# A three-branch decoder trunk: a scan that starts later, values that meet other scores, and four transposes in one bank

## The chip, the cores and the metric

The kernel runs on one core of a Trainium2 chip. The metric is device time in microseconds (us) of one execution. The core has TensorE (PE, matmuls, with PEld for its weight loads), VectorE (DVE), ScalarE (ACT), GpSimd (POOL) and SyncE (SP), and DMA queues that SP, ACT and POOL issue to. Each engine works through its own list of instructions in order and waits where a tile isn't ready.

## What is computed

Two layers, each on a stream x of 256 tokens by 1024 channels. One combined projection of the normalised stream feeds three causal mixers; each has its own SiLU gate path, is projected back, and the three are merged by sigmoid gates, projected and added to x. Cut to what matters:

```python
for layer in range(2):
    h = rms_norm(x, norm_w[layer])
    proj = einsum('bsd,de->bse', h, w_in[layer])             # 1024 -> 12832
    (a_xbc, a_z, a_dt, b_q, b_k, b_v, b_z, c_q, c_k, c_v, c_f, c_z, gates) = split(proj)
    y_a = mamba2_branch(a_xbc, a_z, a_dt, ...)               # conv, scan in chunks of 128, 16 heads of 64 in 4 groups
    y_b = sliding_window_branch(b_q, b_k, b_v, b_z, ...)     # window 128, 16 heads, 4 kv heads, sinks
    y_c = forgetting_attention_branch(c_q, c_k, c_v, c_f, c_z, ...)   # 16 heads, decaying scores
    branch = einsum('bsiw,iwd->bsid', stack(y_a, y_b, y_c), w_proj[layer])
    g = sigmoid(gates + gate_bias[layer])
    x = x + einsum('bsd,de->bse', sum(g * branch), w_out[layer])
return rms_norm(x, final_norm_w)

def scan_of_a_group(x, dt, a, B, C):                         # two chunks
    x_dt = x * dt
    decay = exp(a_cum[l] - a_cum[s]) where l >= s
    y_diag = (C B^T * decay) x_dt                            # inside a chunk
    y_off  = C * state of the chunk before * exp(a_cum)      # across the chunks
    return y_diag + y_off
```

All is float32. The kernel's names: branch 0 is the scan (mamba2), branch 1 the sliding-window attention (swa), branch 2 the forgetting attention (fox). z is a branch's gate path.

## The kernel before, in words

**Matmuls.** Every projection is computed in a split of float32 into a high and a low part: three products (hi·hi, lo·hi, hi·lo) per 128 rows of the contraction. Weights stream from memory in pieces of 512 KB on SP's queue into tiles `raw`; ACT makes `hi` (L291) and DVE makes `lo` (L292), a few pieces ahead of PE (AHEAD 4). The smaller products (scores, values, transposes, the scan) are plain float32.

**The order of PE** is written by a planner that runs while the program is built. A list `ops` holds the projections of a layer in a fixed order: the sequence in the main loop from L1255 on, with `heavy` (eight convolution pieces of the scan's inputs), `lights` (one lighter piece behind each), `z1` (gate paths), and `gates_proj(br)` (two merge gates `g` and two output projections `p` of a branch). Between projections, and in the middle of wide ones, `pump` (L149) takes steps of generators from the list `waiting`: one generator for each quad of attention heads (`swa_quad`, `fox_quad`, both through `attn_quad`), and one `ssd_group` (L853) for each of the scan's four groups. A generator yields a number (planner microseconds until its next step), a condition, a token's name, or `Half(...)`. The planner's clock advances by an estimate for each matmul; `pump` takes at most 1.35 us of steps at a time. `Half` marks a step whose matmuls use only half of PE's array (64 columns or 64 rows). Such steps are held until another one is near (`early`, within MEET 5 us), and if one is taken the others that are ready follow without regard to the budget. `drain(br)` runs a branch's generators to their end.

**Other engines** aren't ordered by the planner but by a scheduler that lets whatever is ready go first. Tiles of one tag share a few buffers; a tile gets its buffer in the order of the program's first writers. The tags that matter: `L4` has two buffers (the scan's broadcasts, the fox attention's turned probabilities `two`, the swa's `first`), `L2` eight (gates, `xdt`, the decays and others), `mx` five PSUM banks. Tokens: one for prepared probabilities (`pp`), one for a group between its preparation and the end of its values (`ssd`), two for broadcasts (`bcg`).

**A group of the scan** (`ssd_group`). It waits until all swa generators are gone, takes a `bcg` token, and issues on ACT's queue a broadcast of its four rows of cumulated decay rates to all partitions (L857, 512 KB). After D_BC and with the `ssd` token it transposes its x into `mx` banks, two transposes to a bank, and DVE multiplies each bank by dt into `xdt` (L866). Then DVE and ACT make `ds` (L869, L870), and the decays `dec` (L879, L881) and `cross` (L885, the last reader of the broadcast). D_SSD later PE makes the products of C and B, DVE multiplies the decays by them (L894). The next yield is `Half(D_SSD2)`, and then come 24 matmuls of 64 columns, the group's values (`py`, L906).

**Fox attention** (`attn_quad`). A quad's scores go to four `mx` banks, DVE and ACT make probabilities, six transposes, a pause, six transposes; ACT copies each bank of four (L696) to `two` and one more tile; then value products (L712), which two quads do together, beside the next quad's scores.

**Constants of a layer** (`layer_consts`, `layer_vec`). Layer 1 loads them on POOL's queue at its start, layer 2 on ACT's at the end of layer 1. The rows dt_bias, f_bias, sinks, a_log and d_skip (16 values each) go to one partition (`y.hr`); a matmul with ones spreads them to 128 partitions, ACT copies them to `y.hb`.

**Order of the gates of branch 1.** In layer 1 the gate piece (1,0) is projected early in the layer, (1,1) behind the fifth heavy piece, and the projection (p,0) behind the eighth. In layer 2 gate 0 comes behind the fifth, projection 0 behind the eighth, then gate 1 and projection 1.

Of the kernel before, what the change touches and what calls it, by code (L numbers as in the profile page):

```python
# [13 lines left out]
AF = mybir.ActivationFunctionType  # L14
ALU = mybir.AluOpType

P = 128
# [9 lines left out]
D_GN1, D_GN2, D_CUM, D_H, D_M = 8.0, 13.5, 17.0, (4.8, 6.4), 5.0  # L27
BUDGET = 1.35
T_PP, T_SSD, T_BIAS = 1, 1, 1
D_FOLD = 8.0  # L30
N_RAW, N_SPLIT = 6, 6
AHEAD = 4
# [16 lines left out]
def hybrid_trunk(  # L49
# [17 lines left out]
    def T(tag, shape, dtype=F32, bufs=None):  # L67
        count[0] += 1
        return sb.tile(shape, dtype, tag=tag, name=f"{tag}_{count[0]}",
                       bufs=bufs if bufs is not None else BUFS.get(tag, 1))  # L70
# [8 lines left out]
    def pmx():  # L79
        return PS("mx", 5)  # L80
# [28 lines left out]
    def transpose(o, a, i):  # L109
        clock["t"] += 0.109  # L110
        nc.tensor.transpose(o, a, i)  # L111
# [36 lines left out]
    def pump(budget=BUDGET):  # L148
        t0 = clock["t"]  # L149
        half = False  # L150
        while True:
            over = clock["t"] - t0 >= budget
            if over and not half:
                return
            for m in sorted(waiting, key=lambda m: (m[0], m[1])):
                if ready(m) and (m[5] if over else not early(m)):
                    half = m[5]
                    enter(m)
                    break
            else:  # L160
                return
# [123 lines left out]
    def pin(f):  # L285
        return lambda *a, **k: tc.keep_in_program_order(f(*a, **k))
# [145 lines left out]
    def layer_consts(y, queue):  # L432
        l = y.l
        pdma = pin(queue.dma_start)
        both = T("L1", [88, 2 * P])
        vr, y.hr = both[:, 0:P], both[0:1, P:P + 80]
        pdma(vr[0:64, :], conv_w[l].rearrange("j (u p) -> (j u) p", p=P))
        pdma(vr[64:80, :], conv_b[l:l + 1, :].rearrange("o (u p) -> (o u) p", p=P))
        pdma(vr[80:88, :], ssm_norm_w[l:l + 1, :].rearrange("o (u p) -> (o u) p", p=P))
        if l:  # L440
            y.nwb = T("nwb", [P, D])
            pdma(y.nwb, norm_w[l:l + 1, :].to_broadcast([P, D]))
            pin(nc.gpsimd.tensor_scalar)(y.nwb, y.nwb, -0.5, None, op0=ALU.mult)

        for i, v in enumerate((dt_bias, f_bias, sinks, a_log, d_skip)):
            pdma(y.hr[:, 16 * i:16 * i + 16], v[l:l + 1, :])
        y.vr = vr

    def layer_vec(y):
        p = pmx()  # L450
        transpose(p[:, 0:88], y.vr, ident[:88, :88])
        y.vec = T("vec", [P, 88], bufs=2)
        mm(p[:, 96:176], ones[0:1, :], y.hr, start=True, stop=True)
        y.hb = T("hb", [P, 80], bufs=2)
        pin(act)(y.hb, p[:, 96:176], AF.Copy)
        pin(act)(y.vec[:, 0:80], p[:, 0:80], AF.Copy, scale=0.5)
        pin(act)(y.vec[:, 80:88], p[:, 80:88], AF.Copy, scale=-0.5)
        y.nega = T("nega", [P, 16], bufs=2)
        pin(act)(y.nega, y.hb[:, 48:64], AF.Exp)
        gts = nc.gpsimd.tensor_scalar  # L460
        y.nsink = T("nsink", [P, 16], bufs=2)
        gts(y.nsink, y.hb[:, 32:48], -1.0, None, op0=ALU.mult)
        gts(y.nega, y.nega, -1.0, None, op0=ALU.mult)
        y.dsk = T("dsk", [P, NK], bufs=2)
        for i in range(2):
            r = slice(64 * i, 64 * i + 64)
            nc.gpsimd.tensor_copy(y.dsk[r, :], y.hb[r, 64:80].rearrange("p (j i) -> p i j", i=2)[:, i, :])
# [384 lines left out]

    def ssd_group(y, g):  # L853
        yield lambda: not any(m[2] == 1 for m in waiting)
        yield "bcg"
        bcg = T("L4", [P, 4, S])
        nc.scalar.dma_start(bcg, y.cumd[1, 4 * g:4 * g + 4, :].partition_broadcast(P))  # L857
        yield D_BC
        yield "ssd"
        xdt = T("L2", [P, 2, 256])  # L860
        hs = slice(4 * g, 4 * g + 4)
        for t in range(2):
            p = pmx()
            for j in range(2):
                transpose(p[:, j * P:(j + 1) * P], y.xs[:, 2 * g + j, t * P:(t + 1) * P], ident)
            tt(xdt[:, t, :].rearrange("p (h d) -> p h d", h=4),  # L866
               p[:, 0:256].rearrange("p (h d) -> p h d", h=4), bc(y.dt[:, t, hs], 2, 64), op=ALU.mult)
        ds = T("ds", [P, 4], bufs=2)
        tt(ds, bcg[:, :, P - 1], y.acum[:, 0, hs], op=ALU.subtract)  # L869
        act(ds, ds, AF.Exp)  # L870
        xds = T("L1", [P, 256])
        tt(xds.rearrange("p (h d) -> p h d", h=4), xdt[:, 0, :].rearrange("p (h d) -> p h d", h=4),
           bc(ds, 2, 64), op=ALU.mult)
        decs = []
        for c in range(2):
            tk = slice(c * P, (c + 1) * P)
            dec = T("L2", [P, 4, P])
            for h in range(4):
                stt(dec[:, h, :], bcg[:, h, tk], y.acum[:, c, 4 * g + h:4 * g + h + 1], negtri,  # L879
                    op0=ALU.subtract, op1=ALU.add)  # L880
            act(dec, dec, AF.Exp)  # L881
            decs.append(dec)

        cross = T("L2", [P, 4, P])
        act(cross, bcg[:, :, P:S], AF.Exp)  # L885
        decs.append(cross)
        yield D_SSD
        tokens["bcg"] += 1

        p = pmx()  # L890
        mm(p[:, 0:S], y.bcT[:, g, 0:P], y.bcT[:, 4 + g, :], start=True, stop=True)
        mm(p[:, S:3 * P], y.bcT[:, g, P:S], y.bcT[:, 4 + g, P:S], start=True, stop=True)
        for dec, c in zip(decs, (0, 2, 1)):
            tt(dec, dec, bc(p[:, c * P:(c + 1) * P], 1, 4), op=ALU.mult)  # L894
        yield Half(D_SSD2)

        py = pmx()
        for c in range(2):
            for j in range(2):
                o = py[:, S * j + P * c:S * j + P * c + P]  # L900
                for s in range(c + 1):
                    for i in range(2):
                        h = 2 * j + i
                        hc = slice(64 * h, 64 * h + 64)
                        a, b = (xdt[:, c, hc], decs[c][:, h, :]) if s == 0 else (xds[:, hc], cross[:, h, :])
                        mm(o[64 * i:64 * i + 64, :], a, b, start=(s == 0), stop=(s == c))  # L906
        for j in range(2):
            u = 2 * g + j
            stt(y.xs[:, u, :], y.xs[:, u, :], y.dsk[:, u:u + 1], py[:, S * j:S * j + S], op0=ALU.mult, op1=ALU.add)
        yield D_SSD3  # L910
        tokens["ssd"] += 1
# [337 lines left out]
    for y in layers:  # L1249
# [27 lines left out]
        def gates_proj(br):  # L1277
            def g(b):
                c = 512 * b
                op(cols(C_G + D * br + c, 512), u_gate(y, br, c, 0), u_gate(y, br, c, 1))  # L1280

            def p(b):
                c = 512 * b
                if b == 0 and br != 0:
                    op(None, lambda y=y: split_late(y, br))
                i = sub([(0, w_proj[l, br, :, c:c + 512])], 512)
                if br == 0:
                    op(i, u_proj_normed(y, c, 0), u_proj_normed(y, c, 1))
                else:
                    op(i, u_proj(y, br, c, 0), u_proj(y, br, c, 1))  # L1290
            seq = [(g, 0), (p, 0), (g, 1), (p, 1)]
            if br == 1 and l == 0:

                seq = [(g, 0), (g, 1), (p, 0), (p, 1)]
            if br == 0:

                seq = [(lambda b: z1(C_ZA, 0, b), b) for b in range(4)] + [(g, 0), (g, 1), (p, 0), (p, 1)]
            return [lambda f=f, b=b: f(b) for f, b in seq]

        gp = gates_proj(1)  # L1300
        if l == 0:
            v, cv0, cv1 = cols(C_BV), cols(C_CV), cols(C_CV + 256)
            op(v, *(u_bv(y, t, first) for t in range(2)))
            op(None, lambda: layer_consts(y0, nc.gpsimd))
            op(None, lambda: launch(9, normalize(y0), 0.0))
            op(cv0, u_cv(y, 0, 0), u_cv(y, 0, 1))
            op(cv1, u_cv(y, 256, 0), u_cv(y, 256, 1))
            gp.pop(0)()
            op(None, lambda: tables(fin["rope"]))
            op(None, lambda: normalized(y0))  # L1310
        else:
            cv0, v = cols(C_CV, 512), cols(C_BV)
            op(None, lambda: drain(5))
            op(cv0, u_cv(y, 0, 0))
            op(v, u_bv(y, 0))
            op(None, lambda: drain(6))
            op(cv0, u_cv(y, 0, 1))
            op(v, u_bv(y, 1))
        op(rcols(C_BK), *u_bk(y))
        for g in range(4):  # L1320
            op(rcols(C_BQ + 256 * g), *u_bq(y, g))
# [242 lines left out]
```

## Time and profile before

| | |
|---|---|
| three runs | 1197.9, 816.55, 814.36 us; median 816.55 |
| the profiled execution | 815.95 us, span 814.2 us, granted PE clock 0.998 |
| PE busy | 803.2 us, 99% |
| DVE, ACT, POOL busy | 684.4, 534.4, 157.4 us |
| DMA | 170.35 MB, mean 209 GB/s |
| scan broadcasts | 8 of 512 KB, issued at 165.51, 165.89, 185.41, 202.14 in layer 1 and 554.28, 554.65, 574.77, 593.05 in layer 2 |

A profile page gives busy times for each engine, and then the span in 40 slices, one digit each, in tenths of busy time. The waits view lists what an engine waited for: total us, times, longest. Timelines list instructions: start, duration, engine, line, operation, output from inputs, array tile, shape; a bracket at the end is the idle time before and what ended it. Matmul durations overlap, so on PE the distance from one start to the next counts. L107 and L111 are the helpers through which all matmuls and all transposes go; a row's names and shapes tell which step it is.

### The profile page before, as it was taken

What the parts mean: (1) busy time and instruction counts of PE and PEld (TensorE: products, weight loads), DVE (VectorE), ACT (ScalarE), POOL (GpSimd) and SP (SyncE); (2) the same over time, 40 slices, a digit from 0 to 9 for tenths busy, and PEclk for the clock granted to TensorE, in tenths of its full rate; (3) what the DMA queues carried; (4) which work ended last, traced back from release to release, by engine and by line L of the source; (5) the groups of instructions that cost most, each with busy time, mean ns of one, the idle gap of its engine ahead of it and who ended that gap; (6) DMA issues with size and microseconds to landing.
All of it is one profiled execution on the core that took longest, in us unless ns stands there. A gap on an engine that the chain in (4) does not pass through costs nothing.

```text
span 814.2 us, 14891 instructions
## 1 busy us (share of the span) xinstructions
PE 803.2 (99%) x5182; PEld 714.8 (88%) x5182; DVE 684.4 (84%) x1420; ACT 534.4 (66%) x1144; POOL 157.4 (19%) x227
## 2 busy tenths in 40 slices
PE   8999999999999999999999999999999999999996
PEld 7998988888898988888999898888888889888896
DVE  6879899979999798686786889997999878869865
ACT  7777768855776786543666676885657768745452
POOL 3066113120210201030005612313003110001100
PEclk9999999999999999999999999999999999999999
DMA  9898888687875554667689888769877565566632
GB/s 310 274 261 194 226 219 205 198 237 229 253 207 167 167 165 158 213 213 241 216 266 267 189 227 239 185 198 244 256 238 201 156 173 164 170 231 217 210 104 77
DMA packets 138708, 170.35 MB, mean 209 GB/s; under 512 B 9346, under 2 KB 106362, under 8 KB 138634
## 3 DMA queue, kind: packets, MB, share of 16 engines
q1 hardware_dynamic: 114960, 140.53, 55.7%
q0 software_dynamic: 12928, 12.63, 9.6%
q10 hardware_dynamic: 10746, 16.24, 6.5%
q8 instruction: 41, 0.67, 0.3%
q14 instruction: 33, 0.27, 0.1%
HBM read 154.63 MB, written 2.16 MB: 193 GB/s over the span
## 4 chain that ended last, share of the span: by engine, by line
PE 88%; DVE 4%; DMA 4%; ACT 2%; issue 2%; SPq 0%; DVEq 0%; ACTq 0%
PE mm L107 76%; PE mx L107 9%; PE mx L111 3%; DMA L<-cumd 3%; DVE lo L292 2%; DVE L L830 1%; DMA raw<-in_w_in_dram 1%; DVE L L292 0%; ACT L L827 0%; DVE L L894 0%; ACT hi L291 0%; DVE L L879 0%; DVE L L1084 0%; ACT L L881 0%; ACT L L1087 0%
## 5 line engine op out<-in xcount | busy, mean ns | idle before, releaser
L107 PE MATMUL mm<-L,hi 128*128 128x512 f32 x1056 | 355.4, 387 | 1.1 <-ACT qt L491 1.0
L292 DVE TENSOR_TENSOR lo<-raw,hi 128x1024 fp32r<-128x1024 f32 (+2 forms) x276 | 313.9, 1157 | 46.1 <-ACT hi L291 44.3
L107 PE MATMUL mm<-hi,L 128*128 128x512 f32 (+2 forms) x1168 | 303.8, 349 | 0.1
L291 ACT ACTIVATE hi<-raw 128x1024 fp32r<-128x1024 f32 (+2 forms) x276 | 264.6, 980 | 57.0 <-PE mm L107 44.0
L107 PE MATMUL mm<-L,lo 128*128 128x256 f32 x1056 | 266.7, 273 | 0.0
L107 PEld LDWEIGHTS mm<-hi,L 128*128 128x128 f32 x1168 | 206.0, 190 | 22.5 <-issue 1.3
L107 PEld LDWEIGHTS mm<-L,hi 128*128 128x128 f32 x1056 | 195.5, 190 | 29.1 <-issue 4.6
L107 PEld LDWEIGHTS mm<-L,lo 128*128 128x128 f32 x1056 | 202.3, 192 | 5.1
L107 PE MATMUL mm<-lo,L 128*128 128x512 f32 (+2 forms) x584 | 201.6, 347 | 0.0
L107 PEld LDWEIGHTS mm<-lo,L 128*128 128x128 f32 x584 | 110.4, 190 | 10.6
L492 POOL DMA_DIRECT2D L<-L x68 | 59.3, 888 | 192.0 <-ACT L L491 133.2
L830 DVE SCALAR_TENSOR_TENSOR L<-L,vec,L 128x255 f32<-128x255 f32 (+2 forms) x96 | 46.2, 482 | 1.7
L1053 POOL TENSOR_SCALAR_AFFINE_SELECT bias<-bias 128x128 f32<-128x128 f32 x64 | 29.0, 488 | 86.2 <-DMA bias<-cumd 60.7
L490 ACT ACTIVATE L<-mm 128x256 f32<-128x256 f32 x84 | 31.8, 378 | 20.9 <-PE mm L107 17.0
L1087 ACT ACTIVATE L<-L 128x512 f32<-128x512 f32 x24 | 15.1, 630 | 35.7 <-DVE L L1084 31.3
L656 ACT ACTIVATE pp<-pp,nm 128x128 f32<-128x128 f32 x64 | 28.2, 441 | 10.2 <-DVE nm L650 10.2
L492 POOL DMA_DIRECT2D qt<-L x16 | 13.8, 859 | 88.4 <-ACT qt L491 46.9
L614 ACT ACTIVATE pp<-pp,nm 128x128 f32<-128x128 f32 x32 | 12.6, 394 | 24.9 <-DVE nm L619 24.1
L491 ACT ACTIVATE L<-mm 128x256 f32<-128x256 f32 x68 | 25.9, 381 | 0.8 <-DMA L<-L 0.8
L925 ACT ACTIVATE L<-L 128x256 f32<-128x256 f32 x48 | 19.7, 411 | 9.7 <-DVE L L483 9.5
L1120 POOL TENSOR_TENSOR L<-L,L 128x512 f32<-128x512 f32 x8 | 11.9, 1494 | 70.9 <-DVE L L1119 70.9
L836 ACT ACTIVATE L<-L 128x256 f32<-128x256 f32 x32 | 13.4, 418 | 17.8 <-DVE L L830 17.6
(211 smaller groups left out, 910.5 us busy)
## 6 DMA issues: line engine op xcount, KB each, us to landing
raw<-in_w_in_dram SPq DMA_DIRECT2D x191, 512.0 KB, 4.7
raw<-in_w_proj_dram SPq DMA_DIRECT2D x48, 512.0 KB, 5.4
L<-L POOLq DMA_DIRECT2D x72, 128.0 KB, 4.9
raw<-in_w_out_dram SPq DMA_DIRECT2D x16, 512.0 KB, 4.6
bias<-cumd ACTq DMA_DIRECT2D x16, 256.0 KB, 5.5
L<-cumd ACTq DMA_DIRECT2D x8, 512.0 KB, 3.6
L<-in_gate_bias_dram ACTq DMA_DIRECT2D x12, 256.0 KB, 5.9
qt<-L POOLq DMA_DIRECT2D x16, 128.0 KB, 5.3
```

What stands on the lines that cost most here:

```text
L107: nc.tensor.matmul(o, a, b, **kw)
L111: nc.tensor.transpose(o, a, i)
L291: keep(act)(hi, src, AF.Copy)
L292: keep(tt)(lo, src, hi.bitcast(F32), op=ALU.subtract)
L490: act(halves(lo), ordered(p[:, S:2 * S]), AF.Copy)
L491: last = act(halves(out), ordered(p[:, 0:S]), AF.Copy)
L492: nc.gpsimd.dma_start(out, lo, accum_op=ALU.add)
L656: act(pp[:, i, sl], pp[:, i, sl], AF.Exp, scale=-1.0, bias=nm[:, e:e + 1], accum_out=sums[:, e:e + 1])
L830: stt(a[:, s:S], x_[:, 0:S - s], y.vec[:, 16 * j + u:16 * j + u + 1], a[:, s:S], op0=ALU.mult, op1=ALU.add)
L925: act(th, o, AF.Tanh, scale=0.5)
L1053: nc.gpsimd.affine_select(out=bias[:, i, dst], in_=bias[:, i, src], compare_op=ALU.is_ge, fill=NEG, base=0, pattern=[[-1, P]], channel_mul ...
L1087: finish(act(g, g, AF.Tanh, scale=0.5))
```

## The change

Five edits:

- Group 0 of the scan, and only that, yields `D_SCAN` = 18 planner us after the swa branch has gone, before it takes its token.
- The values of a group: where they were a `Half` after D_SSD2, that becomes a plain pause, and behind it a `Half` with a condition. It is met when a step of branch 2 that is a `Half` (fox scores) is ready, or when `D_MEET` = 12 planner us have gone by. In `pump`'s order, `Half` steps of other branches than the scan come last, so that the scan's values stand before the scores.
- Layer 2: gate (1,0) is put to the front, behind the projection of v, and branch 1 has the order gate 0, gate 1, projection 0, projection 1, as in layer 1.
- The four transposes of a group go to one `mx` bank, and one multiply of 512 makes `xdt`.
- The five bias rows are broadcast by DMA into `y.hb` (128 partitions of 16 values each), without the ones matmul and the copy. The tile of the constants shrinks.

```diff
-            for m in sorted(waiting, key=lambda m: (m[0], m[1])):
+            for m in sorted(waiting, key=lambda m: (m[5] and m[2] != 0, m[0], m[1])):
...
-        both = T("L1", [88, 2 * P])
-        vr, y.hr = both[:, 0:P], both[0:1, P:P + 80]
+        vr = T("L1", [88, P])
+        y.hb = T("hb", [P, 80], bufs=2)
...
-            pdma(y.hr[:, 16 * i:16 * i + 16], v[l:l + 1, :])
+            pdma(y.hb[:, 16 * i:16 * i + 16], v[l:l + 1, :].to_broadcast([P, 16]))
...
-        mm(p[:, 96:176], ones[0:1, :], y.hr, start=True, stop=True)
-        y.hb = T("hb", [P, 80], bufs=2)
-        pin(act)(y.hb, p[:, 96:176], AF.Copy)
...
         yield lambda: not any(m[2] == 1 for m in waiting)
+        if g == 0:
+            yield D_SCAN
         yield "bcg"
...
+        p = pmx()
         for t in range(2):
-            p = pmx()
             for j in range(2):
-                transpose(p[:, j * P:(j + 1) * P], y.xs[:, 2 * g + j, t * P:(t + 1) * P], ident)
-            tt(xdt[:, t, :].rearrange("p (h d) -> p h d", h=4),
-               p[:, 0:256].rearrange("p (h d) -> p h d", h=4), bc(y.dt[:, t, hs], 2, 64), op=ALU.mult)
+                n = 2 * t + j
+                transpose(p[:, n * P:(n + 1) * P], y.xs[:, 2 * g + j, t * P:(t + 1) * P], ident)
+        tt(xdt.rearrange("p t (h d) -> p t h d", h=4), p.rearrange("p (t h d) -> p t h d", t=2, h=4),
+           bc(y.dt[:, :, hs], 3, 64), op=ALU.mult)
...
-        yield Half(D_SSD2)
+        yield D_SSD2
+        limit_ = clock["t"] + D_MEET
+        yield Half(lambda: clock["t"] >= limit_ or any(m[2] == 2 and m[5] and ready(m) for m in waiting))
...
-            if br == 1 and l == 0:
+            if br == 1:
...
             op(cv0, u_cv(y, 0, 1))
             op(v, u_bv(y, 1))
+            gp.pop(0)()
         op(rcols(C_BK), *u_bk(y))
```

More of the change, by code (lines that the diff above doesn't have):

```diff
@@ L29 @@
 T_PP, T_SSD, T_BIAS = 1, 1, 1
+D_MEET = 12.0
+D_SCAN = 18.0
 D_FOLD = 8.0
```

## Prediction

> **What bounds the kernel now.** I read the page first, its busy shares and the 40 slices.
>
> ```profile
> span 814.2 us, 14891 instructions
> PE 803.2 (99%) x5182; PEld 714.8 (88%) x5182; DVE 684.4 (84%) x1420; ACT 534.4 (66%) x1144; POOL 157.4 (19%) x227
> PE   8999999999999999999999999999999999999996
> DVE  6879899979999798686786889997999878869865
> PEclk9999999999999999999999999999999999999999
> ```
>
> TensorE (PE) is busy in every slice at a full clock. So the time is the length of PE's instruction list plus the few places in which PE waits. The whole kernel has 814.2 − 803.2 = 11.0 us that PE isn't busy, start and end included: an edit that leaves the matmuls alone can't win more than about that. The second view, what PE waited for, says how little of it is inside.
>
> ```profile
> PE mm L107 <- ACT qt L491: 1.0, 2, 0.5
> PE mx L107 <- DVE L L894: 0.9, 4, 0.4
> ```
>
> These two rows, 1.9 us together, are the waits that stand in the part of the program that the change reorders. The first is a stall behind the scan's broadcast in each layer, the second the values of the scan's first group, which wait for the decays' multiply (L894). VectorE (DVE) is the engine nearest to PE. In layer 1's scan, by the windows view (columns: window, length, busy of PE, PEld, DVE, ACT, POOL, clock, DMA share, GB/s):
>
> ```profile
> 223.00:243.00 20.00, 20.00 (x149) 17.99 (x149) 19.56 (x54) 14.41 (x37) 2.36 (x10) 1.00 0.68 199
> 263.00:283.00 20.00, 20.00 (x134) 17.99 (x133) 14.67 (x29) 13.72 (x28) 4.23 (x8) 1.00 0.54 157
> ```
>
> DVE has 0.44 us to spare in 20 us at 223 and 5.33 us at 263. PE loses nothing in either.
>
> **The change part by part.** Costs on PE are measured from one start to another, as its records overlap.
>
> *The ones matmul goes.* The five rows of biases are broadcast by DMA; the two matmuls that spread them, and ScalarE's (ACT's) copy, go in each layer.
>
> ```profile
> 63.58 0.44 PE L107 MATMUL mx<-L,ones 1*128 1x80 f32 x2
> 63.96 0.48 PE L107 MATMUL mm<-L,hi 128*128 128x512 f32 x1
> ```
>
> They hold PE for 63.96 − 63.58 = 0.38 us; two layers, **−0.76**. The five DMAs per layer stay five, but each now writes 128 rows of 64 bytes. They stay on POOL's queue in layer 1 and on ACT's in layer 2. The last of the five before:
>
> ```profile
> 20.73 0.48 POOL L286 DMA_DIRECT2D L<-in_d_skip_dram  x1
> ```
>
> The kernel's own broadcasts to 128 rows land like this (KB each, median us from issue to landing):
>
> ```profile
> L<-cumd ACTq DMA_DIRECT2D x8, 512.0 KB, 3.6
> ```
>
> From 20.73 to the reader at 63.58 lie 42.85 us. Lower bound 0. Upper bound: if each of the five took as long as these 512 KB, one after another, 18 us, they would still be covered, so 0 too. ACT's queue in layer 2 has its five at the end of layer 1, a whole normalisation and more ahead. If the cover is gone, the first reader of the biases (layer_vec) and PE behind it would wait.
>
> *The scan's values meet the fox scores.* A group's 24 value matmuls use 64 columns, and every entry into such a mode costs PE a gap. Before, only the first group of layer 1 falls alone, and all four of layer 2 do. Entry alone and a plain matmul:
>
> ```profile
> 213.00 0.38 PE L107 MATMUL mm<-L,hi 128*128 128x512 f32 x1
> 213.31 1.58 PE L107 MATMUL mx<-qt 64*128 64x128 f32 x16
> ```
>
> ```profile
> 190.80 0.38 PE L107 MATMUL mm<-hi,L 128*128 128x512 f32 x1
> 191.01 0.38 PE L107 MATMUL mm<-lo,L 128*128 128x512 f32 x1
> 191.77 1.03 PE L107 MATMUL mx<-L,L 128*64 128x128 f32 x12 [0.38 <-DVE L L894]
> 192.97 0.88 PE L107 MATMUL mx<-L,L 128*64 128x128 f32 x12 [0.16 <-DVE L L894]
> 193.77 0.48 PE L107 MATMUL mm<-hi,L 128*128 128x512 f32 x1
> ```
>
> The 512 wide matmul is followed by its like after 0.21 us (190.80 to 191.01) and by a half-array block after 0.31 (213.00 to 213.31), so an entry costs 0.10. By the planner's rules, walked through by hand, all eight groups now meet scores: five entries fewer, **−0.50**. Between two half modes (columns, then rows) I count a change as full price. The Trainium skill, page "TensorEngine Tiling (Array Packing)", section Tiling Modes (Key Properties), says that changing the mode, and not only the tile, drains TensorE; by it the border inside a merged block is paid too, which is the sum I make; if that border were free the term would be −1.00.
>
> *What the values wait for.* The same rows hold the second row of the waits. Undisturbed, 24 such matmuls take this:
>
> ```profile
> 260.17 1.53 PE L107 MATMUL mx<-L,L 128*64 128x128 f32 x24
> 261.63 0.48 PE L107 MATMUL mm<-L,hi 128*128 128x512 f32 x1
> ```
>
> 261.63 − 260.17 = 1.46. In layer 1 the first group took 193.77 − 191.77 = 2.00, and its start was late by 191.77 − 191.01 − 0.31 = 0.45: together 0.99. In layer 2:
>
> ```profile
> 579.82 0.38 PE L107 MATMUL mm<-lo,L 128*128 128x512 f32 x1
> 580.42 1.04 PE L107 MATMUL mx<-L,L 128*64 128x128 f32 x12 [0.22 <-DVE L L894]
> 581.61 0.88 PE L107 MATMUL mx<-L,L 128*64 128x128 f32 x12 [0.16 <-DVE L L894]
> 582.42 0.48 PE L107 MATMUL mm<-hi,L 128*128 128x512 f32 x1
> ```
>
> 0.60 − 0.31 = 0.29, and 2.00 − 1.46 = 0.54: 0.83. Values that wait up to 12 us more for scores find their decays done: **−1.82**. The three multiplies of one group take some 2 us of DVE, so a few us of cover suffice. Late next would be the scores themselves, for which the list of PE's waits has no row.
>
> *The scan begins later.* Group 0 yields 18 us before it takes its broadcast. Groups 1 to 3 don't; by my walk group 1 passes it, and the order becomes 1, 0, 2, 3. Two of the L4 buffers are free at that time, and a DMA here is issued when its buffer is, not when PE gets there. So I expect the first two broadcasts where they were, on ACT's queue:
>
> ```profile
> 165.51 0.33 ACTq L857 DMA_DIRECT2D L<-cumd  x1
> ...
> 165.89 0.76 ACTq L857 DMA_DIRECT2D L<-cumd  x1
> ```
>
> ```profile
> 172.87 0.16 DVE L869 TENSOR_TENSOR ds<-L,acum 128x4 f32<-128x4 f32 x1 [4.03 <-DMA L<-cumd]
> ```
>
> DVE sits 4.03 us at ds until the broadcast has landed, and behind it are the splits and rope steps that ACT and PE want. PE shows it so:
>
> ```profile
> 173.63 0.38 PE L107 MATMUL mm<-L,hi 128*128 128x512 f32 x1
> 173.85 0.60 PE L111 MATMUL mx<-ident,L 128*128 128x128 f32 x4
> 174.90 0.48 PE L107 MATMUL mm<-L,hi 128*128 128x512 f32 x1 [0.45 <-ACT qt L491]
> ```
>
> Undisturbed, four transposes take 240.66 − 240.30 = 0.36:
>
> ```profile
> 240.30 0.60 PE L111 MATMUL mx<-ident,L 128*128 128x128 f32 x4
> 240.66 0.46 PE L107 MATMUL mm<-L,hi 128*128 128x512 f32 x1
> ```
>
> Here they take 174.90 − 173.85 = 1.05, so 0.69 is stall; the wait's row counts two such places, one in each layer. The transposes of the scan's first group stand there for nothing, as it were. Later they stand in a place in which PE doesn't wait, and the stall has nothing to fill it: +0.36 a layer, **+0.72**. Bounds: if the later ds also removes the block, −0.69 a layer, −1.38; if it stays, +0.72. I take +0.72, since ds needs no transposes and the broadcast has its buffer.
>
> *Shared buffers.* The L4 tag has two buffers, for the broadcasts and for the fox attention's turned probabilities (two). With the scan later, the order of the tag at the end of a layer's scan becomes group 2, fox 0, group 3, fox 1, and fox 1's probabilities need the buffer that fox 0's value products release. Before, it was close already (ACT):
>
> ```profile
> 246.67 0.62 ACT L885 ACTIVATE L<-L 128x512 f32<-128x512 f32 x1
> ...
> 247.76 0.59 ACT L696 ACTIVATE L<-mx 128x512 f32<-128x512 f32 x1
> ```
>
> The last reader of a broadcast ended at 247.29 and the copy into that buffer began at 247.76, 0.47 us later. After, PE has fox 0's first 16 value matmuls to do before the buffer is free:
>
> ```profile
> 255.90 1.52 PE L107 MATMUL mx<-L,L 128*64 128x256 f32 x16
> 257.25 1.47 PE L107 MATMUL mm<-L,L 128*64 128x256 f32 x16
> ```
>
> That is 1.35 us, then two copies of 0.59 before its next 16. Lower bound 0, when the copies fit beside other steps of PE; upper bound 1.35 + 2 × 0.59 = 2.5 us a layer. I take 1.0, nearer to the two copies, **+2.0**.
>
> *Layer 2's order.* Its first gate of branch 1 moves to the front, and both gates of branch 1 stand ahead of its projections, the order that layer 1 has. No PE instruction is added. Cover: layer 1, whose order this is, has PE busy 20.00 of 20 in the windows above. The gate's two tiles of L2 live longer, ahead of the scan; L2 has 8. I take 0, with ±0.5.
>
> *Transposes in one bank.* A group's four transposes keep their count; DVE does one multiply of 512 instead of two of 256. That saves DVE some tenths per group, beside PE. 0.
>
> *DVE moved.* Later prep moves a group's decays out of the window at 223 (0.44 to spare) into the one at 263 (5.33 to spare). Cover: that spare; if it went, the splits (hi, lo) that PE's weights come from would be late, and PE with them. As PE has no wait there now, nothing can be won: 0.
>
> **The sum.** −0.76 − 0.50 − 1.82 + 0.72 + 2.0 = −0.36. The profiled execution took 815.95 us (span 814.2 and 1.75 around it), so 815.6. The median of the three runs shown is 816.55, 0.6 above the profiled one, and the fastest 814.36.
>
> **The rivals.** *A, buffers suffice.* The L4 wait doesn't arise, as PE works on projections while ACT copies: 815.95 − 0.76 − 0.50 − 1.82 + 0.72 = 813.6; if the block at ds goes too, 811.5. For it: PE shows no wait for L4 now. Against: 0.47 us of slack before, and the order gets tighter.
>
> *B, slower.* A broadcast takes the buffer late and a group's whole preparation comes to stand in PE's way. The chain of waits shows the price:
>
> ```profile
> 185.41 4.35 DMA L<-cumd
> ...
> 192.97 0.88 PE mx L107 x12
> ```
>
> From issue to the values' second half 7.6 us. Once in each layer that is +15.1 on A's 813.6: 828.7. It decides when a broadcast is issued less than 7.6 us ahead of the scores that its group meets. For it: only two buffers, and the landing is not hidden if late. Against: the third broadcast, this one, was issued 19.5 us after the second (165.89), and the landing is far less than that.
>
> Slower by over 2% it is from 832.9 on, that is with 9.6 us in each layer. The Trainium skill, page "TensorE: Matmul & The Clock Gate", section Part 1, says that an idle window of about 3.4 us puts the clock to half, and that about 3.4 us of work bring it back; by it each such stall would cost about another 1.7 us (an estimate from the page), 832.1 in all. No run here has PE idle that long inside; the clock's row is 9 throughout.
>
> *C, they don't meet.* The 12 us run out before a score is ready, and the values fall alone: no −0.50, and they don't hold the scores up: 815.95 − 0.76 − 1.82 + 0.72 = 814.1. For it: scores wait for a token of their own. Against: three of layer 1's four met already.
>
> **How the numbers follow.** Forecast (sum with the buffer wait) 0.48, A 0.27, C 0.12, B 0.13. The time is the likeliest's, 815.6; its own range is 814 to 819. The range 812 to 820 holds A nearly whole, C, and the upper bound of the buffer wait (815.95 − 2.36 + 5.0 = 818.6) with a run's own scatter; it leaves out most of B. A measurement of this kernel can tell about 2% from no change, 16.3 us. Faster by that is excluded by the 11.0 us of PE's idle and the 0.76 of removed work, but for 0.01; slower needs B beyond its point, 0.025; the same 0.965.
>
> **What would show it.** Right: no row of ones matmuls; no wait on the multiply of L894's successor; all eight value blocks of 24 beside 16 scores; PE's wait on qt as before or a little longer; a new wait of PE for the copies of the fox probabilities, about 1 us a layer. Order of groups 1, 0, 2, 3. Wrong: PE idle over 5 us in a layer behind a broadcast, or a fall of PE's busy share below 98%.

## The result, and the profile after

The changed kernel took 812.95 us (median of six runs, 812.28 to 814.04), the kernel before 815.52 beside it (median of five; a sixth run, of 1197.9, is left out here and in the ratio). The ratio is 0.9971, 95% interval 0.9959 to 0.9984. So the change wins about 2.4 us (1.3 to 3.3), clear of scatter but far below 2%. The forecast was 815.6, range 812 to 820, "the same" with 0.965.

The profiled execution of the changed kernel took 813.07 us, 2.88 less than that of before. Its page and PE's waits (line numbers differ from those of before by up to five):

```profile
span 811.4 us, 14867 instructions
PE 800.2 (99%) x5178; PEld 714.2 (88%) x5178; DVE 683.8 (84%) x1412; ACT 533.4 (66%) x1142; POOL 172.7 (21%) x227
```

```profile
PE mx L113 <- POOL ident masks.py:199: 1.5, 1, 1.5
PE mx L113 <- DVE L L1128: 1.2, 1, 1.2
PE mm L109 <- ACT L L695: 0.9, 2, 0.5
```

Both old rows are gone: PE no longer waits for L894's multiplies, nor for ACT behind the first broadcast. Two new ones stand in their place. L695 is the copy of the fox attention's turned probabilities, 0.46 us in each layer: the shared buffer that the sum had as +2.0. L1128 is DVE's merge at the end of layer 1: nothing in the prediction had it.

The first group's values now, in layer 1 (PE timeline; start, duration):

```profile
205.71 1.53 PE L109 MATMUL mx<-L,L 128*64 128x128 f32 x24
207.18 1.58 PE L109 MATMUL mx<-qt 64*128 64x128 f32 x16
208.69 0.48 PE L109 MATMUL mm<-L,hi 128*128 128x512 f32 x1
```

24 values in 1.47 us without a pause, then 16 scores: one entry into half modes for both, as forecast. All eight groups stand so, two of them with the 32 value products of a fox pair between.

The broadcast and ds (DVE), where 4.03 us stood before:

```profile
171.82 0.16 DVE L871 TENSOR_TENSOR ds<-L,acum 128x4 f32<-128x4 f32 x1 [2.90 <-DMA L<-cumd]
```

The block is still there but 1.1 us shorter; ACT's idle time before the row behind it fell from 2.77 us to 1.13, and PE doesn't feel it.

### The profile page after: what moved, and what is told of

Same layout as the page of the kernel before. It is cut to its first block, busy times and chain, and to the rows that moved or that the text cites. A ratio compares the mean times of both kernels' runs of the same rounds, so it can differ in the third digit from the quotient of the medians.

```text
span 811.4 us, 14867 instructions
## 1 busy us (share of the span) xinstructions
PE 800.2 (99%) x5178; PEld 714.2 (88%) x5178; DVE 683.8 (84%) x1412; ACT 533.4 (66%) x1142; POOL 172.7 (21%) x227
## 4 chain that ended last, share of the span: by engine, by line
PE 96%; DMA 2%; DVE 1%; ACT 1%; issue 0%; SPq 0%; DVEq 0%
PE mm L109 83%; PE mx L109 10%; PE mx L113 3%; DMA raw<-in_w_in_dram 1%; DMA raw<-in_w_proj_dram 1%; DMA hb<-in_sinks_dram 0%; DVE lo L294 0%; ACT L L695 0%; ACT hi L293 0%; SPq L363 0%; SPq L189 0%; DVE L L1431 0%; DVE L L1127 0%; DVE L L1128 0%; ACT L L1435 0%
## 5 line engine op out<-in xcount | busy, mean ns | idle before, releaser
L294 DVE TENSOR_TENSOR lo<-raw,hi 128x1024 fp32r<-128x1024 f32 (+1 forms) x276 | 313.1, 1153 | 37.8 <-ACT hi L293 36.6
L293 ACT ACTIVATE hi<-raw 128x1024 fp32r<-128x1024 f32 (+1 forms) x276 | 265.6, 981 | 51.1 <-PE mm L109 37.1
L1057 POOL TENSOR_SCALAR_AFFINE_SELECT bias<-bias 128x128 f32<-128x128 f32 x64 | 40.7, 671 | 69.3 <-DMA bias<-cumd 69.2
L1088 DVE TENSOR_TENSOR L<-mm,L 128x512 f32<-128x512 f32 x22 | 15.1, 686 | 16.4 <-DMA L<-in_gate_bias_dram 8.8
L835 ACT ACTIVATE L<-L 128x256 f32<-128x256 f32 x32 | 13.4, 418 | 19.0 <-DVE L L829 18.9
```

Of the source, the lines that this page charges most:

```text
L293: keep(act)(hi, src, AF.Copy)
L294: keep(tt)(lo, src, hi.bitcast(F32), op=ALU.subtract)
L1057: nc.gpsimd.affine_select(out=bias[:, i, dst], in_=bias[:, i, src], compare_op=ALU.is_ge, fill=NEG, base=0, pattern=[[-1, P]], channel_mul ...
L1088: tt(halves(g), p, halves(y.gb), op=ALU.add)
```

## The experiments

Twelve kernels, each timed in five rounds beside the kernel before on the same chip. Ratios are against the kernel before, and gains and losses in us are worked out from them where nothing else is said.

**One edit at a time.** *Bias rows.* The kernel before with this edit alone:

```diff
-            pdma(y.hr[:, 16 * i:16 * i + 16], v[l:l + 1, :])
+            pdma(y.hb[:, 16 * i:16 * i + 16], v[l:l + 1, :].to_broadcast([P, 16]))
...
-        mm(p[:, 96:176], ones[0:1, :], y.hr, start=True, stop=True)
```

> The kernel before with the bias rows broadcast by DMA, and nothing else of the change. Theory 1 (the broadcasts hold up ACT's queue at the end of layer 1): PE gains 0.5 us in each layer at layer_vec, and loses about 1.2 us at the end of layer 1, where four transposes wait for DVE's merge behind a split that ACT makes late; sum about +0.2 us, ratio 1.000 to 1.001, and a row of PE's waits with the merge (DVE L1124 or so) of about 1.2 us. Theory 2 (my prediction: the broadcasts cost nothing): -0.8 to -1.0 us, ratio about 0.999, no such row.

815.8 us, ratio 1.0001 (0.9991 to 1.001). PE's wait at the merge was 0.8 us in its profile (0.98 over an ordinary step). Theory 1 fits, with a smaller wait than its 1.2; the prediction's gain of 0.76 isn't seen, though the interval (−0.7 to +0.8 us) only just leaves it out.

*The meeting.*

```diff
-            for m in sorted(waiting, key=lambda m: (m[0], m[1])):
+            for m in sorted(waiting, key=lambda m: (m[5] and m[2] != 0, m[0], m[1])):
...
-        yield Half(D_SSD2)
+        yield D_SSD2
+        limit_ = clock["t"] + D_MEET
+        yield Half(lambda: clock["t"] >= limit_ or any(m[2] == 2 and m[5] and ready(m) for m in waiting))
```

> The kernel before with only the new condition of the values' Half and the new order in pump. Theory (as predicted): all eight groups' values stand beside fox scores, PE's row of waits for the decays' multiply (0.9 us) goes, the row for qt (1.0 us) stays; -1.8 for the waits and -0.5 for the entries, some 2.3 us less, ratio 0.997. Rival: the values find their scores only because the scan begins later; then some groups still fall alone, the 0.9 us stay at least in part, and the gain is under 1 us.

819.31 us, ratio 1.0039 (1.0027 to 1.0051): slower by 3.2. Both theories fell. Of the rival the mechanism came, not the time: the first group of each layer still falls alone, and part of the wait for the decays' multiply stays (L896). PE's waits of this run:

```profile
PE mm L109 <- DVE lo L294: 1.8, 2, 1.4
PE mx L113 <- POOL ident masks.py:199: 1.5, 1, 1.5
PE mm L109 <- ACT L L698: 1.0, 2, 0.5
PE mm L109 <- ACT qt L493: 1.0, 2, 0.8
PE mx L109 <- DVE L L896: 0.6, 3, 0.3
```

The longest is in layer 2, and DVE's timeline tells why:

```profile
580.07 0.16 DVE L871 TENSOR_TENSOR ds<-L,acum 128x4 f32<-128x4 f32 x1 [1.77 <-DMA L<-cumd]
580.17 1.22 DVE L294 TENSOR_TENSOR lo<-raw,hi 128x1024 fp32r<-128x1024 f32 x1
581.32 1.88 DVE L896 TENSOR_TENSOR L<-L,mx 128x512 f32<-128x512 f32 x3
583.11 1.22 DVE L294 TENSOR_TENSOR lo<-raw,hi 128x1024 fp32r<-128x1024 f32 x1
```

DVE waits 1.77 us for a broadcast, then makes one split and three multiplies of a group's decays. The split that PE wants begins at 583.11 and ends at 584.33; PE goes on at 584.38 after 1.37 us idle. The multiplies that used to hold up their own values now hold up the weights.

*The pause.*

```diff
         yield lambda: not any(m[2] == 1 for m in waiting)
+        if g == 0:
+            yield D_SCAN
```

> The kernel before with only the pause of 18 ahead of group 0's broadcast. Theory 1 (my prediction): ds still blocks DVE at the first broadcast, PE's stall for ACT's qt stays and grows by the 0.36 us of the transposes that filled it, +0.7 us in two layers, ratio 1.001. Theory 2 (what the changed kernel's waits suggest): with the transposes later, ACT and DVE reach ds later, the block shortens to 3 us and PE doesn't feel it: the 1.0 us row goes, -1.4 us, ratio 0.998.

814.83 us, ratio 0.9988 (0.998 to 0.9997). No row of ACT's qt among PE's waits: theory 2, the prediction's step failed. The gain is 1.0 us (0.2 to 1.6). In its profile new waits of PE come along (0.5 for L698, 0.5 for L870, the multiply of a group's transposes by dt, 0.4 for the merge).

*Layer 2's order.*

```diff
-            if br == 1 and l == 0:
+            if br == 1:
...
             op(v, u_bv(y, 1))
+            gp.pop(0)()
```

> The kernel before with only layer 2's branch 1 in layer 1's order. Theory: no instruction more or less, no wait moves: within 0.5 us, ratio 1.000. Rival: the gate's tiles, which live longer, or the other spacing of the projections in layer 2 change which values meet scores there, and the time moves by 0.5 to 1.5 us in either direction.

814.95 us, ratio 0.9993 (0.9984 to 1.0002). The interval holds no change. But the rival is seen in the trace: three of layer 2's four groups of values now stand beside scores, as in layer 1, where none did before.

By their ratios these four sum to +0.1 + 3.2 − 1.0 − 0.6 = +1.7 us. The whole change gives −2.4. The fifth edit, four transposes in one bank, wasn't run alone, so this sum by itself doesn't show that the edits don't add up; the run without the pause, below, does.

**Together.** The pause and the meeting on the kernel before:

> The kernel before with the pause and the meeting together, none of the other three edits. Alone the meeting cost 3.2 us and the pause won 1.0. Theory (the two work together: the pause spaces the groups so that waiting values don't crowd the next group's preparation): 2 to 3 us less than before, ratio about 0.997, no wait for the decays' multiply and none for lo. Rival (effects add up, and layer 2's order is what makes the whole change a gain): 2 us more than before, ratio 1.003.

816.07 us, ratio 1.001 (1.0 to 1.0019), 0.8 us more. Neither: less than the sum of both (+2.2), though hardly by more than the scatter, and not the gain of the whole. And the changed kernel without the pause:

> The changed kernel without the pause of 18 ahead of group 0. Theory (the meeting of values and scores pays only when the groups are spaced by the pause; without it the groups' decays and the splits crowd, as in the run with the meeting alone): some 3 to 4 us more than the changed kernel, 816 to 817, with PE waits for lo and for the decays' multiply. Rival: the loss in that run came from layer 2's old order; then this run stays within 1 us of 813.

817.74 us, ratio 1.0034 (1.0023 to 1.0045). Theory, 0.7 over its upper end: without the pause the other four edits lose 2.8 us on before, with it they win 2.4. So the pause is worth 5 us here and 1.0 alone.

And with layer 2's old order:

> The changed kernel with layer 2's branch 1 in its old order. In the run with the pause and the meeting alone, layer 1 was 1.4 us shorter than before and layer 2 1.5 us longer, with waits of 1.4, 0.3, 0.5 and 0.4 us in the blocks of values and scores. Theory (in layer 2 the meeting works only with the new order, which shifts the scan against the fox scores): 3 to 4 us more than the changed kernel, all of it in layer 2, about 816. Rival (those waits were due to two transposes to a bank and the second multiply; the order is worth its own 0.8 us): 813.5 to 814.

815.22 us, ratio 1.0 (0.9991 to 1.0009): 2.3 more than the changed kernel, not 3 to 4. To see where, each profiled run is cut at the eight transposes that open layer 2 (405.71 in the profile of before); layer 2 counts from there to the start of the last matmul:

| kernel | layer 1, us | layer 2, us |
|---|---|---|
| before | 405.71 | 401.96 |
| meeting alone | 406.34 | 404.39 |
| pause alone | 407.22 | 399.79 |
| order alone | 404.64 | 401.28 |
| meeting and pause | 404.33 | 403.48 |
| changed, old order | 403.64 | 402.91 |
| changed, no pause | 406.74 | 402.08 |
| changed | 405.06 | 399.77 |

These are single executions. Layer 1 of "order alone" runs the same program order as before and differs by 1.07 us, and layer 1 of "changed, old order" runs that of the changed kernel and differs by 1.42; so a difference under about 1.4 us says nothing here. Above that: in layer 2, with the old order, the meeting costs time with the pause or without it, and the old order costs 3.1 us in layer 2 of the changed kernel.

The table also shows what wasn't asked of it: layer 2 of the pause alone is as short as that of the changed kernel (399.79 and 399.77 us). In these profiles the other four edits together win nothing there that the pause doesn't win by itself; in layer 1 they are 2.2 us ahead of it (405.06 and 407.22). The changed kernel without the meeting wasn't run, so whether the meeting earns anything in the whole stays open; so does the one bank for the transposes. For that there is only a bound: the changed kernel with the old order differs from the run with meeting and pause by the bias rows and the one bank, and is 0.8 us shorter (1.0 against 1.001), with intervals that overlap.

Back to layer 2 with the old order. One place carries 1.4 of the 3.1 us (PE timeline of the changed kernel with the old order, then DVE's):

```profile
626.91 1.53 PE L109 MATMUL mx<-L,L 128*64 128x128 f32 x24
628.37 0.93 PE L109 MATMUL mx<-qt 64*128 64x128 f32 x8
630.49 1.43 PE L109 MATMUL mx<-qt 64*128 64x128 f32 x8 [1.19 <-issue]
```

```profile
628.38 1.23 DVE L294 TENSOR_TENSOR lo<-raw,hi 128x1024 fp32r<-128x1024 f32 x1
629.52 0.86 DVE L913 SCALAR_TENSOR_TENSOR L<-L,dsk,mx 128x256 f32<-128x256 f32 x2
```

The last eight scores come only after DVE's L913 has read the values out of their bank (629.52 + 0.86 = 630.38), and L913 stood behind a split of 1.23 us. Values and four banks of scores are all five `mx` banks; with one more bank in use the scores would wait for the values' own. Which bank it was isn't shown, so this cause is argued, not proven; the wait itself is in both runs with the old order and the pause (1.36 us over an ordinary step in each) and in none with the new order.

**The two new waits.** For the end of layer 1, the timelines of ACT before and after (its queue issues layer 2's constants there):

```profile
358.90 0.23 ACTq L286 DMA_DIRECT2D L<-in_sinks_dram  x1
...
359.84 1.06 ACT L291 ACTIVATE hi<-raw 128x1024 fp32r<-128x1024 f32 x1 [7.07 <-DMA L<-in_a_log_dram]
```

```profile
356.87 0.33 ACTq L288 DMA_DIRECT2D hb<-in_sinks_dram  x1
357.24 0.44 ACTq L288 DMA_DIRECT2D hb<-in_a_log_dram  x1
357.73 1.36 ACTq L288 DMA_DIRECT2D hb<-in_d_skip_dram  x1
359.19 1.06 ACT L293 ACTIVATE hi<-raw 128x1024 fp32r<-128x1024 f32 x1 [8.25 <-DMA hb<-in_sinks_dram]
```

ACT computes nothing for 8.25 us instead of 7.07; 4.8 us of before and 4.3 of after lie between the issues of the second and the third row, so most of this pause is not the change's. The issue of the last row took 1.36 us; one row to one partition took 0.26. That length is of this execution: in the five other profiles with the broadcasts on ACT's queue the last row took 0.44 to 0.50, and in one of them it is the plain row of the gate biases, right behind, that took 1.39. Behind ACT's split stands DVE's, behind that the merge, and behind that PE, which lost 1.17 us:

```profile
363.16 0.69 DVE L1128 TENSOR_TENSOR L<-L,L 128x512 f32<-128x512 f32 x1
```

```profile
363.90 0.66 PE L113 MATMUL mx<-ident,L 128*128 128x128 f32 x4 [1.17 <-DVE L L1128]
```

The test is one word:

```diff
-        ... lambda: layer_consts(layers[1], nc.scalar))
+        ... lambda: layer_consts(layers[1], nc.gpsimd))
```

> The changed kernel with layer 2's constants on POOL's queue instead of ACT's. Theory (ACT, held up 8.3 us at issuing these DMAs, makes a split late, and the merge and four transposes of PE wait for it): PE's wait of 1.2 us at 363.9 goes, about 1.3 us less than the changed kernel, 811.6. Rival: the wait is due to the weights' stream or the merge itself at that place; then it stays, and the time is 813. A second rival: POOL's own merges stand behind the DMAs and the wait only changes its name.

811.9 us, ratio 0.996 (0.9947 to 0.9972), about 1 us less than the changed kernel by the medians, though the two intervals overlap. The wait is gone, and PE has no row in its place. Theory. The word moves all the constants of layer 2, not the five rows alone: ACT's idle time there falls to 5.43 us, below that of before. The other way to take it away, with the ones matmul back:

> The changed kernel with the bias rows spread by the ones matmul again. Theory: PE has the matmul and its mode change twice more, +1.0 us, and doesn't have the 1.2 us wait at the end of layer 1 (0.1 to 0.2 of it stay, as before): within 0.5 us of the changed kernel. Rival: the wait is there without the broadcasts too; then about 814, 1 us more.

812.84 us, ratio 0.9963 (0.9951 to 0.9976), no wait there. Theory: within the scatter, the bias edit wins at layer_vec in the whole change what it loses at the end of layer 1. The size of that wait varies: 0.4 to 1.3 us over an ordinary step in the six profiles that have the broadcasts on ACT's queue; of the kernels without them one (the pause alone) had 0.6 there, so the place is tight anyway.

For the shared buffer, three of L4 with fewer L1 to make room, and the control:

```diff
-    BUFS = dict(..., L4=2, L2=8, L1=14, ...)
+    BUFS = dict(..., L4=3, L2=8, L1=11, ...)
```

> The changed kernel with three buffers for L4 (L1 cut from 14 to 11 to make room). Theory (fox 1's turned probabilities wait for the buffer that fox 0's value products release): PE's two waits of 0.53 us inside the value blocks (249.5 to 251.6 and the same in layer 2) go, about -1.0 us against the control with eleven L1. Rival: the copies are late because ACT is busy; then the waits stay.

> Control for the run with three L4 buffers: the changed kernel with eleven L1 buffers and two of L4. The two waits of 0.53 us in the value blocks are there as in the changed kernel; the time is what fewer L1 buffers cost, 0 to 3 us over 813.

814.51 us (ratio 0.9992, 0.9981 to 1.0002) against 814.26 (0.9986, 0.9977 to 0.9995): no gain in time, though the wait is gone as forecast. After, and with three buffers (PE):

```profile
248.31 2.83 PE L109 MATMUL mx<-L,L 128*64 128x128 f32 x40
251.60 1.58 PE L109 MATMUL mm<-L,L 128*64 128x256 f32 x16 [0.46 <-ACT L L695]
```

```profile
250.25 2.83 PE L109 MATMUL mx<-L,L 128*64 128x128 f32 x40
252.91 1.47 PE L109 MATMUL mm<-L,L 128*64 128x256 f32 x16
```

251.60 − 248.31 = 3.29 becomes 252.91 − 250.25 = 2.66. But with a free buffer the first broadcast went out at 152.26 instead of 164.99, and PE waited elsewhere, among the sliding window's values:

```profile
163.16 1.16 PE L109 MATMUL mm<-L,bias 128*64 128x256 f32 x10 [0.81 <-DVE L L678]
```

So the fox attention's tile was taken out of L4 instead, on top of the constants on POOL's queue; the first broadcast then stays where it was (164.57), and the last of layer 2 goes out at 614.85 instead of 635.40:

```diff
-                        two = T("L4", [P, 2, 512])
+                        two = [T("L2", [P, 512]) for _ in range(2)]
```

> The changed kernel with layer 2's constants on POOL's queue, and the fox attention's turned probabilities in two tiles of L2 instead of one of L4. Theory: the two waits of 0.53 us in the value blocks go as well, about 1.0 us less than with the constants on POOL alone, 810.8. Rival: L2's eight buffers run short in their turn (gates, decays) and a wait in another place takes it back: 812 or more.

810.08 us, ratio 0.993 (0.9918 to 0.9943). PE has one row of waits left, at the start of the program:

```profile
PE mx L113 <- POOL ident masks.py:199: 1.5, 1, 1.5
```

That is 2.9 us better than the changed kernel and 5.7 better than before, the fastest of all. Against the run with the constants on POOL it is 1.8 us by the medians; the two waits in the value blocks account for 1.3 of it, and where the rest comes from isn't shown.

## Why the prediction was right, and where not

The verdict was right for the reason given: PE's list sets the time, and 11 us of idle is all there is. The time was forecast less well. 812.95 is inside 812 to 820, which was wide enough to hold most of rival A (811.5 to 813.6), but outside 814 to 819, the range of the sum itself. What came is a mixture of the two: the buffer wait of the sum, at two thirds, with the lower bound of the scan's term. The sum was −0.36 and the profile says −2.88. It is luck that it wasn't further off: the scan's term was 2.1 us too high, and the bias rows' DMAs, at 0, were 1.2 too low. Term by term:

- **Ones matmul, −0.76.** Measured −1.03. The prediction counted from the first ones matmul; but the transpose ahead of it also took longer to its successor (0.17 us, and 0.03 without the ones matmul). Ahead of the two rows of before that the prediction shows stands the first of these; the other two are of the changed kernel:

```profile
63.41 0.24 PE L111 MATMUL mx<-ident,L 88*128 88x88 f32 x1
```

```profile
63.34 0.24 PE L113 MATMUL mx<-ident,L 88*128 88x88 f32 x1
63.37 0.46 PE L109 MATMUL mm<-L,hi 128*128 128x512 f32 x1
```

  63.96 − 63.41 = 0.55 against 0.03, 0.52 a layer.
- **The DMAs of the bias rows, 0.** Wrong: +1.2 in this profile. The prediction bounded the landing, which was never late. It didn't price the issue: the instructions that issue these DMAs stand in ACT's own list, ahead of a split that PE needs. Up to 0.9 of it may be the one long issue of 1.36 us.
- **The meeting, −0.50 and −1.82.** Both are seen in the whole change: all eight meet, no row for the multiply. The border inside a merged block is paid, as the sum had it: the scores begin 1.47 us after the values, and a plain matmul behind values alone 1.46 (prediction, 260.17 to 261.63). But the step gave −1.82 to the meeting, and the meeting by itself leaves 0.6 us of that wait and costs 3.2 us. The pause by itself takes the wait away: in its run all eight groups have 24 values without a break. Layer 1's first group does so with no scores beside it, and three of layer 2's groups meet scores without the new condition; here are that group and the first of these three (PE, the pause alone):

```profile
201.16 1.53 PE L109 MATMUL mx<-L,L 128*64 128x128 f32 x24
202.62 0.48 PE L109 MATMUL mm<-L,hi 128*128 128x512 f32 x1
```

```profile
612.25 1.58 PE L109 MATMUL mx<-qt 64*128 64x128 f32 x16
613.76 1.53 PE L109 MATMUL mx<-L,L 128*64 128x128 f32 x24
```

  In layer 1 of that run no group meets scores; so, by these rows, what the meeting adds to the pause is the price of the entries.
- **"The scan begins later", +0.72.** Wrong in sign. The prediction took the block at ds for the cause and expected it to stay. It stayed, shorter, but PE's stall went, because ACT's order around it changed. ACT before, and after:

```profile
173.06 0.20 ACT L870 ACTIVATE ds<-ds 128x4 f32<-128x4 f32 x1 [2.77 <-DVE ds L869]
...
174.48 0.37 ACT L491 ACTIVATE qt<-mm 128x256 f32<-128x256 f32 x1
```

```profile
170.50 0.39 ACT L490 ACTIVATE qt<-mm 128x256 f32<-128x256 f32 x1
172.02 0.20 ACT L872 ACTIVATE ds<-ds 128x4 f32<-128x4 f32 x1 [1.13 <-DVE ds L871]
```

  The eviction that PE waited for (it ended at 174.85, PE went on at 174.90) stood behind ds and stands ahead of it now. Both stalls went, 0.69 and about as much in layer 2: −1.4, the other bound that was given, and the lower end of rival A. Why the scheduler put the eviction first isn't settled by these runs. The pause alone leaves no stall in either layer; the order alone leaves 0.4 us in layer 2, the meeting alone 0.4 and 1.0. In layer 1 of the order alone, where nothing is changed, only 0.1 of it is left, so part of it may be chance.
- **Shared buffers, +2.0.** Right mechanism, two thirds of the size: 251.60 − 248.31 − 2.66 = 0.63 us a layer, +1.3. The prediction had two copies ahead of PE's next products; PE went on at 251.60, after the first of these two:

```profile
250.95 1.08 ACT L695 ACTIVATE L<-mx 128x512 f32<-128x512 f32 x2 [2.15 <-PE mx L109]
```

- **Layer 2's order, 0 ± 0.5.** Wrong in the whole: alone it wins 0.6, which its interval can't tell from 0, but without it the changed kernel is 2.3 us slower. The term was priced by layer 1, which has this order and no wait; the runs show that what it is worth depends on the other edits.

With these sizes: −1.03 − 0.50 − 1.82 − 1.4 + 1.3 + 1.2 = −2.3; the 0.6 left to −2.88 is below what two single profiles can tell (two pairs differed by 1.07 and 1.42 where nothing was changed).

Rivals B and C didn't come: no idle of PE behind a broadcast, and all values meet.

## What to carry to other kernels

- A DMA costs the engine that issues it, not only its landing: see what stands behind the issue on that engine's list, and who waits for it. Moving a layer's constants to an engine that nobody waited for took away a wait of 1.2 us, and about 1 us of the time, for one word.
- Edits of an order don't add up. Here the pause wins 1.0 us alone and 5 in the whole change. Price them together, and test the whole without each one as well as each one alone: the meeting costs 3.2 us alone, and as the whole wasn't run without it, what it is worth there isn't known.
- A wait for a shared buffer is taken away by moving the late user to another tag; adding a buffer also let an earlier user start sooner (152.26 instead of 164.99), and that moved a wait elsewhere.

## What was not expected of the hardware

- How soon a successor starts depends on what it is: a transpose of 88 rows was followed after 0.17 us by a matmul on one row, and after 0.03 us by a full one. That the change of array mode is the cause isn't shown.
- Issuing a broadcast of 16 values to 128 partitions held ACT's queue for 0.33 to 0.50 us and once for 1.36, one row to one partition for 0.23 to 0.29.
